# Feed-forward matmuls as two 64-row tiles of TensorE, two weight units at a time

## The chip, the core and the metric

The kernel runs on one core of a Trainium2 chip. The metric is the device time of one execution in microseconds (us). TensorE (PE) multiplies a stationary operand of up to 128 rows by 128 columns, loaded by an instruction of its own (LDWEIGHTS), with a moving operand of up to 512 columns; the result is added up in a bank of PSUM (2 KB per partition, here 512 float32). ScalarE (ACT) and VectorE (DVE) read the banks; GpSimd (POOL) works on SBUF only. SyncE (SP) issues the DMAs.

## The reference

Two layers, each: a SwiGLU feed-forward, a mixer of three attentions, a second SwiGLU feed-forward. There are 256 tokens of 1024 channels, and the inner width of the feed-forward is 2816.

```python
def swiglu(h, w1, w3, w2):
    return (jax.nn.silu(h @ w1) * (h @ w3)) @ w2
...
for l in range(DEPTH):
    x = x + 0.5 * swiglu(rms_norm(x, ffn1_norm[l]), ffn1_w1[l], ffn1_w3[l], ffn1_w2[l])
    ...                                   # mixer: projections, three branches, x = x + mixed @ w_out[l]
    x = x + 0.5 * swiglu(rms_norm(x, ffn2_norm[l]), ffn2_w1[l], ffn2_w3[l], ffn2_w2[l])
```

## The kernel before

**Weights.** All weights stream through one list of units of 1 MB (128 partitions x 2048 float32). A unit is loaded by SP into one of 3 `raw` buffers, and split into a high part `hl[:, 0]` (ACT, L138) and a low part `hl[:, 1]` (DVE, L144), in two halves, in one of 4 `hl` buffers. A product of float32 precision is then the sum of three matmuls: high by high, high by low, low by high. `unit()` takes the next unit of the list and makes sure that it and the first half of the next are split; `tick()` is called between pieces of matmul work and emits further splits (`fill`) and one step of each side task. Each engine runs its instructions in the order in which they were emitted.

**Feed-forward, first part (w1 and w3).** `fform(i)` does one unit: 128 columns of w1 and 128 of w3. The weights are stationary (128 rows of the contraction, 128 columns), the transposed activations `xT` move. For each of the two banks (b = 0 for w1, 1 for w3) and each of 8 blocks k of the contraction there are two matmuls: one of 512 columns (weights high, by the activations' high and low parts of all 256 tokens) and one of 256 columns (weights low, by the activations' high part). So a unit has 32 matmuls: 16 couples of 512 and 256 columns. `fdrain` then adds the two halves of each bank (ACT copy L478, DVE add L479), scales on POOL (L480), and in later ticks applies Silu (ACT L485), multiplies (DVE L487) and splits the result into high and low (ACT L489, DVE L491) as `uT`. In the very first feed-forward the units 0 and 1 are done elsewhere and `fform` runs from 2 to 21; in the other three, units 0 and 1 are done token by token (`tform`, then the transposes of `tr_task`), `fform` runs from 2 to 21 too, and after unit 2 `rs_bcast` transposes the norm's scale into a bank of tag `ta`.

**Feed-forward, second part (w2), and the mixer's output.** `wide_out` multiplies stationary activations (128 rows, 128 tokens) by moving weights (512 columns). For each unit u and each half t of the tokens, `wide_burst` does 12 matmuls of 512 columns into the two banks of t (h = 0, 1). The last two units are held back and done bank by bank, so that each bank finishes early. w2 has 11 units (9 in `wide_burst`, 2 held), the mixer's output 4 (2 and 2).

**PSUM.** Eight banks in two tags of four, given out in rotation: `acc` for the accumulators, `ta` for transposes and some others. `fform` takes two `acc` banks per unit, so that two units can be in flight.

Of the kernel before, what the change touches and what calls it, by code (L numbers as in the profile page):

```python
# [6 lines left out]
F32 = mybir.dt.float32  # L7
# [20 lines left out]
S2_BUFS = 31  # L28
FIRST_R = 2

# [15 lines left out]
def body(tc, T):  # L46
# [3 lines left out]
    with ctx:  # L50
# [21 lines left out]

# [1 line left out]
        units = []  # L74
# [95 lines left out]

# [1 line left out]
        tasks = []  # L172
# [28 lines left out]

# [1 line left out]
        x = cst.tile([128, 2, D], F32, name="x")  # L203
# [163 lines left out]
        def mm(out, lhsT, rhs, start, stop):  # L367
            PE.matmul(out=out, lhsT=lhsT, rhs=rhs, start=start, stop=stop, skip_group_check=True)  # L368

# [43 lines left out]
        def wide_out(first, lhs, nu, done):  # L413
            accs = {}
            hold = []
            for u in range(nu):
                hl = unit()
                if u >= nu - 2:
                    hold.append((u, hl))
                    continue  # L420
                for t in range(2):
                    if u == 0:
                        accs[t] = (acc_t(), acc_t())
                    wide_burst(accs[t], lhs, u, hl, t, u == 0, False)
                    tick()
            for t in range(2):
# [9 lines left out]

        def wide_burst(acc, lhs, u, hl, t, start, stop):
            for kk in range(2):
                s, e = start and kk == 0, stop and kk == 1
                for w in range(2):  # L440
                    for h in range(2):
                        mm(acc[h], lhs(0, u, kk, t), hl[:, w, kk * 1024 + h * 512:kk * 1024 + h * 512 + 512],
                           s and w == 0, False)
                for h in range(2):
                    mm(acc[h], lhs(1, u, kk, t), hl[:, 0, kk * 1024 + h * 512:kk * 1024 + h * 512 + 512], False, e)

# [1 line left out]
        def ffn(norms, after, prefetch, first=None, out=None):  # L448
# [44 lines left out]
            def fform(i):  # L493
                hl = unit()
                acc = [(at_t() if first is not None and i == 3 else acc_t()) for _ in range(2)]
                for b in range(2):
                    o = acc[b].rearrange("p (w t n) -> p w t n", w=2, t=2)
                    for k in range(8):
                        a = k * 256 + b * 128
                        both = xT[:, :, :, k, :].rearrange("p t w n -> p w t n")  # L500
                        mm(o, hl[:, 0, a:a + 128], both, k == 0, False)
                        mm(o[:, 0], hl[:, 1, a:a + 128], xT[:, :, 0, k, :], False, k == 7)
                    if b == 0:
                        tick()
                if i == (FIRST_R if first is not None else 2):
                    rs_bcast()
                    if first is not None:
                        for j in range(2):
                            drains[j] = run(fdrain(j, first[j][0][:, :256], first[j][1][:, :256]))
                        for j, a in held:  # L510
                            drains[j] = run(fdrain(j, a))
                if "x" in rs_b:
                    drains[i] = run(fdrain(i, acc))
                else:
                    held.append((i, acc))
                tick()

            us, drains, held = {}, {}, []
            if first is None:
                h2 = [unit(), unit()]  # L520
                for t in range(2):
                    finish(norms[t, 0])
                    finish(norms[t, 1])
                    for i in range(2):
                        us[i, t] = tform(i, h2[i], t)
                        tick(t == 0)
                utr = spawn(tr_task(us), 2)
            for i in range(2, NB):
                fform(i)
                if i == 4:  # L530
                    prefetch()
                    if first is not None:
                        load_consts()
                    if first is None:
                        finish(utr)

# [17 lines left out]

# [1 line left out]
        def mixer(l, norms, after, prefetch):  # L556
# [6 lines left out]

            # ---- evacuations of the projections
            sg, cn, rl, nqk, nav, gvt, ssr = {}, {}, {}, {}, {}, {}, {}
# [94 lines left out]

            # ---- shared by the two softmax attentions
            yT = {}
# [28 lines left out]

            # ---- neighbourhood attention
            naT = {}
# [89 lines left out]

            # ---- latent attention
            mq, mk, mv, mr = {}, {}, {}, {}
# [146 lines left out]

            # ---- gated linear attention
            gqk = {}
# [152 lines left out]

            # ---- projections, with the three mixers running beside them
            m_tk = dense8(512, ev_m, norms)
# [103 lines left out]

# [1 line left out]
        def spawner(ap, into, params_of=None):  # L1195
# [39 lines left out]
def _rel_index():  # L1235
    """Row offset, column offset and window test of (block, query, key) in the order of the bands."""
    j, q, p = np.arange(4)[:, None, None], np.arange(64)[:, None], np.arange(128)
# [102 lines left out]
```

## Time and profile before

| | us |
|---|---|
| median of 3 runs (1270.18 to 1270.63) | 1270.34 |
| span of the profiled execution, first to last instruction | 1267.6 |
| PE busy in it (share) | 1253.1 (99%) |
| PE weight loads busy | 1074.4 (85%) |
| DVE busy | 894.0 (71%) |
| ACT busy | 711.9 (56%) |
| POOL busy | 221.3 (17%) |

The profiled execution's own time is its span and what the runtime puts around it, which the profile does not show; the median of the runs is 2.7 us above the span. PE is busy almost throughout, but a matmul's record lasts longer than the step from it to the next one, since matmuls are pipelined: how fast PE goes is read from the starts of long groups of matmuls and their counts.

### The profile page before, as it was taken

How to read it: one execution, taken by the hardware profiler on the slowest of the kernel's cores; microseconds unless marked ns; L12 is line 12 of the kernel's file. 1: busy time of each engine (PE TensorE's matmuls, PEld its weight loads, DVE VectorE, ACT ScalarE, POOL GpSimd, SP SyncE). 2: the span in 40 equal slices, each digit the busy share in tenths (PEclk: the TensorE clock that was granted, in tenths of full speed). 3: DMA queues.
4: the chain of work that ended last, by engine and by line, in shares of the span. 5: the costliest groups of instructions: out<-in, count | busy, mean ns of one | idle time of the engine just before them, and what ended most of it. 6: DMA issues, size and time to landing. Idle time of an engine off the chain costs nothing.

```text
span 1267.6 us, 18330 instructions
## 1 busy us (share of the span) xinstructions
PE 1253.1 (99%) x7124; PEld 1074.4 (85%) x7124; DVE 894.0 (71%) x1382; ACT 711.9 (56%) x1315; POOL 221.3 (17%) x169
## 2 busy tenths in 40 slices
PE   8999999999999999999999999999999999999998
PEld 7888788889988898888898888888899788988887
DVE  5888736678766878886378886466886567788852
ACT  6555536667665366555365564356686644665541
POOL 0322101132011112220012220021322020122200
PEclk9999999999999999999999999999999999999999
DMA  7655644552543545556355556346526434555561
GB/s 301 222 180 187 241 158 158 203 194 87 196 166 133 200 166 185 185 196 232 133 186 203 195 195 235 113 173 225 167 90 207 163 134 170 196 199 182 186 230 34
DMA packets 37751, 228.34 MB, mean 180 GB/s; under 512 B 5712, under 2 KB 6864, under 8 KB 13088
## 3 DMA queue, kind: packets, MB, share of 16 engines
q1 hardware_dynamic: 37488, 227.09, 50.5%
q8 instruction: 56, 0.92, 0.3%
q14 instruction: 31, 0.25, 0.1%
q0 software_dynamic: 32, 0.07, 0.0%
q10 hardware_dynamic: 144, 0.00, 0.0%
HBM read 224.00 MB, written 1.05 MB: 178 GB/s over the span
## 4 chain that ended last, share of the span: by engine, by line
PE 88%; DVE 7%; ACT 4%; issue 1%; DMA 0%; DVEq 0%; ACTq 0%
PE acc L368 79%; DVE hl L144 6%; PE ta L368 6%; ACT hl L138 2%; ACT s L478 1%; PE ta L689 1%; PE ta L259 1%; DVE s L487 1%; PE ta L776 0%; DVE aT L1017 0%; PE ta L1172 0%; DMA gcol<-in_gcol 0%; PE ta L674 0%; ACT aT L1016 0%; PE ta L608 0%
## 5 line engine op out<-in xcount | busy, mean ns | idle before, releaser
L144 DVE TENSOR_TENSOR hl<-raw,hl 128x1024 fp32r<-128x1024 f32 (+2 forms) x422 | 568.0, 1385 | 101.7 <-ACT hl L138 91.4
L138 ACT ACTIVATE hl<-raw 128x1024 fp32r<-128x1024 f32 (+2 forms) x422 | 417.2, 1041 | 110.2 <-PE acc L368 93.5
L368 PE MATMUL acc<-xT,hl 128*128 128x512 f32 (+1 forms) x2768 | 475.6, 334 | 0.6 <-DVE s L479 0.6
L368 PEld LDWEIGHTS acc<-xT,hl 128*128 128x128 f32 x2768 | 417.8, 188 | 55.7 <-DVE s L479 0.9
L368 PE MATMUL acc<-hl,xT 128*128 128x512 f32 (+2 forms) x1728 | 369.0, 369 | 0.0
L368 PEld LDWEIGHTS acc<-hl,xT 128*128 128x128 f32 x1728 | 299.8, 188 | 45.7 <-issue 2.1
L368 PE MATMUL acc<-hl,s 128*128 128x512 f32 x1344 | 310.9, 391 | 1.5 <-DVE s L479 1.5
L368 PEld LDWEIGHTS acc<-hl,s 128*128 128x128 f32 x1344 | 250.8, 188 | 54.4 <-DVE s L479 1.9
L480 POOL TENSOR_TENSOR s<-s,rsb 128x512 f32<-128x512 f32 x80 | 111.8, 1397 | 355.7 <-DVE s L479 355.7
L489 ACT ACTIVATE s<-s 128x256 fp32r<-128x256 f32 x82 | 34.2, 418 | 172.4 <-DVE s L487 172.4
L479 DVE TENSOR_TENSOR s<-acc,s 128x256 f32<-128x256 f32 x158 | 59.6, 419 | 58.5 <-ACT s L478 58.5
L569 POOL TENSOR_TENSOR sm<-sm,mhalf 128x4 f32<-128x4 f32 (+2 forms) x24 | 36.7, 1531 | 202.7 <-DVE sm L573 196.0
L280 POOL TENSOR_TENSOR sm<-sm,mhalf 128x1 f32<-128x1 f32 x12 | 14.2, 1182 | 298.5 <-DVE sm L279 298.5
L478 ACT ACTIVATE s<-acc 128x256 f32<-128x256 f32 x158 | 50.6, 372 | 0.0
L242 ACT ACTIVATE s<-ta 128x512 fp32r<-128x512 f32 (+1 forms) x46 | 22.9, 531 | 39.9 <-PE ta L689 19.9
L243 DVE TENSOR_TENSOR s<-ta,s 128x512 fp32r<-128x512 f32 (+1 forms) x46 | 26.6, 604 | 24.4 <-ACT s L242 24.1
L368 PE MATMUL ta<-s,s 64*64 64x128 f32 (+3 forms) x720 | 41.0, 265 | 2.1 <-ACT s L1026 2.1
L368 PEld LDWEIGHTS ta<-s,s 64*64 64x64 f32 (+2 forms) x720 | 32.1, 144 | 12.4 <-issue 5.9
L262 ACT ACTIVATE xT<-ta,gain 128x128 fp32r<-128x128 f32 x80 | 22.8, 369 | 35.1 <-PE ta L259 35.1
L485 ACT ACTIVATE s<-s 128x256 f32<-128x256 f32 x82 | 34.2, 418 | 10.9 <-POOL s L480 0.2
L546 DVE SCALAR_TENSOR_TENSOR x<-acc,x 128x512 f32<-128x512 f32 (+1 forms) x20 | 11.3, 579 | 39.7 <-PE acc L368 39.7
L491 DVE TENSOR_TENSOR s<-s,s 128x256 fp32r<-128x256 f32 x82 | 34.0, 415 | 1.9 <-ACT s L489 1.9
(158 smaller groups left out, 652.4 us busy)
## 6 DMA issues: line engine op xcount, KB each, us to landing
raw<-in_l_f_w SPq DMA_DIRECT2D x130, 1024.0 KB, 4.8
raw<-in_l_in_g SPq DMA_DIRECT2D x16, 816.0 KB, 4.4
raw<-in_l_in_late SPq DMA_DIRECT2D x8, 1024.0 KB, 4.8
raw<-in_l_out SPq DMA_DIRECT2D x8, 1024.0 KB, 4.7
raw<-in_l_in_m SPq DMA_DIRECT2D x4, 1024.0 KB, 4.8
raw<-in_l_in_gr SPq DMA_DIRECT2D x4, 1024.0 KB, 4.8
raw<-in_l_in_r SPq DMA_DIRECT2D x4, 1024.0 KB, 4.8
raw<-in_l_in_nv SPq DMA_DIRECT2D x4, 1024.0 KB, 5.0
```

Of the source, the lines that this page charges most:

```text
L138: ACT.activation(out=hls[j][:, 0, sl], in_=raws[j][:, sl], func=AF.Copy)
L144: DVE.tensor_tensor(out=hl[:, 1, sl], in0=r[:, sl], in1=hl[:, 0, sl].bitcast(F32), op=ALU.subtract)
L242: ACT.activation(out=hi, in_=ps, func=AF.Copy)
L243: DVE.tensor_tensor(out=lo, in0=ps, in1=hi.bitcast(F32), op=ALU.subtract)
L368: PE.matmul(out=out, lhsT=lhsT, rhs=rhs, start=start, stop=stop, skip_group_check=True)
L478: ACT.activation(out=g[:, j, :], in_=a[j][:, 256:], func=AF.Copy)
L479: DVE.tensor_tensor(out=g[:, j, :], in0=a[j][:, :256], in1=g[:, j, :], op=ALU.add)
L480: POOL.tensor_tensor(out=g, in0=g, in1=rb[:, None, :].to_broadcast([128, 2, 256]), op=ALU.mult)
L485: ACT.activation(out=g[:, 0, :], in_=g[:, 0, :], func=AF.Silu)
L489: ACT.activation(out=o[:, 0, :], in_=g[:, 0, :], func=AF.Copy)
L491: DVE.tensor_tensor(out=o[:, 1, :], in0=g[:, 0, :], in1=o[:, 0, :].bitcast(F32), op=ALU.subtract)
L569: POOL.tensor_tensor(out=r[:, :n], in0=ss[:, :n], in1=mhalf[:, :n], op=ALU.pow)
```

## The change

`mm` now returns its instruction, and a new helper `duo(P, Q)` issues matmuls in halves: each matmul of 128 contraction rows becomes two of 64 rows, one on rows 0 to 63 and one on rows 64 to 127 of the array. P and Q are two lists of runs with banks of their own. In the first pass the lower row tile does P's runs and the upper one Q's, alternating instruction by instruction; in the second pass they change sides, so that every bank gets both halves of its contraction, and never from both tiles at once. Between the passes a POOL memset of one element (`dot`, L393) waits for the last matmuls of the first pass in a pair of banks, and the second pass there waits for the memset.

`fform_pair(i)` gives `duo` two units (i and i+1) with two banks each, four banks of one tag, `ta` and `acc` in turn. `wide_out` gives it the two token halves of one unit, for all units that are not held back, and swaps their order from unit to unit. In the first feed-forward units 2 and 3 stay with `fform`, and pairs run from 4; in the others from 2, and there `rs_bcast` and the transposes of `tr_task` now stand together behind the first pair. Ticks: four per pair (two per unit before), four per w2 unit (two before).

```diff
         def mm(out, lhsT, rhs, start, stop):
-            PE.matmul(out=out, lhsT=lhsT, rhs=rhs, start=start, stop=stop, skip_group_check=True)
+            return PE.matmul(out=out, lhsT=lhsT, rhs=rhs, start=start, stop=stop, skip_group_check=True).ins
+        HALF = (slice(0, 64), slice(64, 128))
+        dot = cst.tile([1, 4], F32, name="dot")
+        def duo(P, Q, between=None):
+            gate = {}
+            for second in (False, True):
+                for n, pair in enumerate(zip(*((Q, P) if second else (P, Q)))):
+                    last = [None, None]
+                    for i in range(len(pair[0][0])):
+                        for r in range(2):
+                            ops, start, stop = pair[r]
+                            out, lhsT, rhs = ops[i]
+                            last[r] = mm(out, lhsT[HALF[r]], rhs[HALF[r]], start and not second and i == 0,
+                                         stop and second and i == len(ops) - 1)
+                            if second and i == 0:
+                                tc.add_manual_dep(last[r], gate[n], SYNC, reason="the other row tile's run in this bank")
+                    if not second:
+                        g = POOL.memset(dot[:, n:n + 1], 0.0).ins
+                        for r in range(2):
+                            tc.add_manual_dep(g, last[r].name, SYNC, reason="both row tiles' runs")
+                        gate[n] = g.name
+                    if between is not None and not (second and n == len(P) - 1):
+                        between()
...
-                for t in range(2):
-                    if u == 0:
+                if u == 0:
+                    for t in range(2):
                         accs[t] = (acc_t(), acc_t())
-                    wide_burst(accs[t], lhs, u, hl, t, u == 0, False)
-                    tick()
+                P, Q = (wide_runs(accs[t], lhs, u, hl, t) for t in range(2))
+                duo(*((Q, P) if u % 2 else (P, Q)), between=tick)
+                tick()
...
+            def fform_pair(i):
+                runs, accs = [], []
+                for j in (i, i + 1):
+                    hl = unit()
+                    acc = [at_t() if i // 2 % 2 == 0 else acc_t() for _ in range(2)]
...
+                duo(*runs, between=tick)
+                if i == 2:
+                    rs_bcast()
+                    finish(utr)
+                for j in range(2):
+                    drains[i + j] = run(fdrain(i + j, accs[j]))
+                tick()
...
-            for i in range(2, NB):
-                fform(i)
+            if first is not None:
+                for i in (2, 3):
+                    fform(i)
+            for i in range(2 if first is None else 4, NB, 2):
+                fform_pair(i)
```

**Place 1, PE, second feed-forward of layer 0, behind the transposes of the norm's scale (`ta<-idt`).** Before, one bank of one unit after the other; a row is the line, the bank written, the two operands with their buffer numbers, and the output's size:

```order
L466 MATMUL ta_4399<-idt_73,s2_4350 128x128 [waits DVE_49]
L368 MATMUL acc_4416<-xT_74,hl_4251 128x512 [waits Activation_49]
L368 MATMUL acc_4416<-xT_74,hl_4251 128x256
L368 MATMUL acc_4416<-xT_74,hl_4251 128x512
L368 MATMUL acc_4416<-xT_74,hl_4251 128x256
```

Now, at the same place:

```order
L498 MATMUL ta_5387<-idt_73,s2_5231 128x128
L367 MATMUL ta_5410<-xT_74,hl_5236 128x512 [waits Activation_49]
L367 MATMUL ta_5415<-xT_74,hl_5275 128x512 [waits Activation_49]
L367 MATMUL ta_5410<-xT_74,hl_5236 128x256 [waits DVE_49]
L367 MATMUL ta_5415<-xT_74,hl_5275 128x256 [waits DVE_49]
L367 MATMUL ta_5410<-xT_74,hl_5236 128x512
L367 MATMUL ta_5415<-xT_74,hl_5275 128x512
```

Two units (`hl_5236`, `hl_5275`) and two banks alternate, each instruction with half the rows, and the second unit has to be split from the second instruction on.

**Place 2, PE, the first w2 unit of the same feed-forward.** Before, the two banks of one token half alternate:

```order
L368 MATMUL acc_5354<-xT_74,hl_5267 128x256
L368 MATMUL acc_5405<-hl_5319,s2_4404 128x512 [waits DVE_49]
L368 MATMUL acc_5406<-hl_5319,s2_4404 128x512 [waits DVE_49]
L368 MATMUL acc_5405<-hl_5319,s2_4404 128x512
L368 MATMUL acc_5406<-hl_5319,s2_4404 128x512
```

Now the passes; these are the end of the first pass and the start of the second:

```order
L367 MATMUL acc_6943<-hl_6774,s2_5395 128x512
L367 MATMUL acc_6945<-hl_6774,s2_5395 128x512
L367 MATMUL acc_6944<-hl_6774,s2_5392 128x512 [waits Pool_49]
L367 MATMUL acc_6942<-hl_6774,s2_5392 128x512
L367 MATMUL acc_6944<-hl_6774,s2_5392 128x512
```

The second pass of this unit begins with a wait for POOL, 24 instructions (two groups of six couples) behind the unit's start.

**Place 3, POOL, the end of w1/w3 and the start of w2 in the same feed-forward.** Before:

```order
L480 TENSOR_TENSOR s2_5295<-s2_5295,rsb_4393 128x512 [waits DVE_49,Pool_49]
L480 TENSOR_TENSOR s2_5347<-s2_5347,rsb_4393 128x512 [waits DVE_49,Pool_49]
L480 TENSOR_TENSOR s2_5399<-s2_5399,rsb_4393 128x512 [waits DVE_49,Pool_49]
L280 TENSOR_TENSOR sm_5808<-sm_5710,mhalf_81 128x1 [waits DVE_49]
```

Now:

```order
L393 MEMSET dot_84 1x1 [waits PE_49,Pool_49] x2
L512 TENSOR_TENSOR s2_6930<-s2_6930,rsb_5385 128x512 [waits DVE_49]
L512 TENSOR_TENSOR s2_6936<-s2_6936,rsb_5385 128x512 [waits DVE_49]
L393 MEMSET dot_84 1x1 [waits PE_49,Pool_49] x18
L279 TENSOR_TENSOR sm_7583<-sm_7485,mhalf_81 128x1 [waits DVE_49]
```

The memset that lets the first w2 unit's second pass start stands behind the scaling (L512, L480 before) of the last two w1/w3 units.

## Rows read from the trace of the kernel before

**Rows 1.** Page, part 1: engine, busy us, share of the span, instructions.
```profile
PE 1253.1 (99%) x7124; PEld 1074.4 (85%) x7124; DVE 894.0 (71%) x1382; ACT 711.9 (56%) x1315; POOL 221.3 (17%) x169
```

**Rows 2.** Waits of PE over the whole execution: us, times, longest.
```profile
PE ta L368 <- ACT hl L337: 6.0, 1, 6.0
PE ta L368 <- ACT s L1026: 2.1, 2, 1.1
PE acc L368 <- DVE s L479: 2.1, 2, 1.5
PE ta L1172 <- DVE s L1163: 0.4, 2, 0.2
```

**Rows 3.** Timeline of PE, 469 to 640 us: start, length, engine, group, count.
```profile
469.92 106.98 PE L368 MATMUL acc<-xT,hl 128*128 128x512 f32 x608
576.73 54.60 PE L368 MATMUL acc<-hl,s 128*128 128x512 f32 x240
631.17 0.60 PE L259 MATMUL ta<-idt,x 128*128 128x128 f32 x4
```

**Rows 4.** Timeline of PE, 426 to 457 us: the mixer's output.
```profile
430.96 14.20 PE L368 MATMUL acc<-hl,xT 128*128 128x512 f32 x60
445.00 0.60 PE L259 MATMUL ta<-idt,x 128*128 128x128 f32 x4
```

**Rows 5.** Windows, 470 to 576 us: busy (count) by engine, PEclk, DMA.
```profile
core 0: us, PE busy (x) PEld busy (x) DVE busy (x) ACT busy (x) POOL busy (x), PEclk, DMA share, GB/s
470.00:576.00 106.00, 106.00 (x606) 92.90 (x605) 88.49 (x114) 62.75 (x116) 26.39 (x19) 1.00 0.54 187
```

**Rows 6.** Timeline of PE, latent attention's scores; then two shorter stretches of it.
```profile
294.22 1.47 PE L368 MATMUL acc<-xT,hl 128*128 128x256 f32 x11
295.53 2.89 PE L368 MATMUL ta<-s,s 128*128 128x256 f32 x24
298.35 0.50 PE L368 MATMUL acc<-xT,hl 128*128 128x256 f32 x2
...
296.33 0.51 PE L368 MATMUL ta<-s,s 64*128 64x256 f32 x4
...
296.33 0.63 PE L368 MATMUL ta<-s,s 64*128 64x256 f32 x6
```

**Rows 7.** Timeline of PE, gated linear attention: a burst of 64 by 64 tiles.
```profile
1010.70 0.89 PE L368 MATMUL ta<-s,s 64*64 64x128 f32 x24
1011.52 3.05 PE L368 MATMUL acc<-hl,xT 128*128 128x512 f32 x12
```

**Rows 8.** Timeline of all engines, 576 to 582 us: the end of w1/w3.
```profile
576.77 0.64 ACT L478 ACTIVATE s<-acc 128x256 f32<-128x256 f32 x2
577.17 0.76 DVE L479 TENSOR_TENSOR s<-acc,s 128x256 f32<-128x256 f32 x2 [0.76 <-ACT s L478]
578.07 1.34 POOL L480 TENSOR_TENSOR s<-s,rsb 128x512 f32<-128x512 f32 x1 [4.21 <-DVE s L479]
```

**Rows 9.** Groups of POOL: busy us, mean ns of one.
```profile
L300 POOL MEMSET ones<- 128x1 f32 x1 | 0.1, 98 | 0.0
```

**Rows 10.** Timeline of PE, the first feed-forward's change from w1/w3 to w2.
```profile
44.15 90.14 PE L368 MATMUL acc<-xT,hl 128*128 128x512 f32 x512 [0.57 <-DVE s L479]
134.12 2.88 PE L368 MATMUL acc<-hl,s 128*128 128x512 f32 x12
138.49 52.07 PE L368 MATMUL acc<-hl,s 128*128 128x512 f32 x228 [1.49 <-DVE s L479]
```

**Rows 11.** Page, part 5: weight loads of two groups, mean ns in the middle.
```profile
L368 PEld LDWEIGHTS acc<-hl,s 128*128 128x128 f32 x1344 | 250.8, 188 | 54.4 <-DVE s L479 1.9
```

## What the change will do: the prediction

> **What bounds the kernel now.** The page first: PE is busy for 99% of the span, the next engine for 71% [rows 1]. The list of PE's waits confirms it: some 11 us in all, most of it once at the start [rows 2]. So the time is the number of matmuls times the step from one to the next, and the steps are what the change touches. They are read from starts in PE's timeline, not from busy time. In w1/w3 the 608 matmuls that start at 469.92 end where the next group starts, at 576.73 [rows 3]: 106.81 us for 304 couples of 512 and 256 columns, 0.3514 us a couple. In w2, 240 matmuls of 512 columns take 631.17 - 576.73 = 54.44 us, 0.2268 us each [rows 3]; in the mixer's output 60 take 14.04 us, 0.234 us each [rows 4]. The granted clock is 1.00 [rows 5], the 2.4 GHz level, at which 512 columns alone are 0.2133 us, a couple 0.3200. What is left above the columns is 13 to 21 ns per matmul, and no more than that can be gained in these stretches.
>
> How much of the kernel they are: pairs run 9 times in the first feed-forward and 10 times in each other one, 39 duos of 2 units of 16 couples, 1248 couples x 0.3514 = 438.5 us; w2 has 4 x 9 units of 24 matmuls, 864 x 0.2268 = 196.0 us; the mixers' outputs 96 x 0.234 = 22.5 us. Together 657 us.
>
> **The change, part by part.**
>
> *The step of a row-tiled matmul.* A matmul of 128 rows becomes two of 64 rows with the same columns. If the two run side by side, a slot (the two together) lasts as long as the one did, and nothing is gained in streaming. The trace has such matmuls already: in the latent attention's scores, 64 rows by 128 columns by 256 columns, in two row tiles and two banks. Four of them last 0.51 us from the first start to the last end, six last 0.63 [rows 6]: one more pair costs 0.12 us. Full-height matmuls of 256 columns right before take 295.53 - 294.22 = 1.31 us for 11, 0.119 us each [rows 6]. So two tiles do run side by side, and the step stays the same, gap included: 0.12 against 0.1067 for the columns alone. No row shows 512 columns in row tiles. I take the nearest row, the same matmul width of 128 columns at half the length, and so no change: 0 us. The bounds: the gap goes altogether (0.2133 and 0.3200, worth -52.9 us, worked out below), or all 512-column slots take the slowest step seen, 0.234 (w2: 864 x 0.0072 = +6.2 us; couples at 0.234 + 0.120: 1248 x 0.0026 = +3.2 us).
>
> *Twice the instructions.* There are 3456 more matmuls and as many loads. A slot now has four instructions in 0.176 us on average, 44 ns each. In the gated attention 24 matmuls with their loads start in 1011.52 - 1010.70 = 0.82 us, 17 ns each [rows 7], so issuing them is hidden behind streaming; 0 us. Loads do not bind either: the 256-column pair of tiles has two loads in its 0.12 us.
>
> *Going in and out of row tiling.* The same group of rows prices it. From 295.53 to 298.35, 2.82 us, PE does 12 full matmuls and 6 pairs in turns (6, 3, 6, 3): 18 slots of 0.12 are 2.16, the other 0.66 us are four changes of tiling, 0.165 us each [rows 6]. In the order the changed kernel has 11 row-tiled blocks: one in the first feed-forward, two in each other one (the pair of units 2 and 3, then transposes, then the rest through w2), two in each mixer's output, where transposes of the merge stand after the first quarter of unit 0. 22 changes x 0.165 = **+3.6 us**.
>
> *The gates.* In w1/w3 a pass is 2 x 16 slots, 16 couples or 5.62 us. The first gate's memset is queued on POOL behind the scaling of the two units of the pair before. At the end of w1/w3 (the group that starts at 576.73 [rows 3] is w2) the rows give: copies from 576.77, adds until 577.93, scaling from 578.07 for 1.34 us [rows 8], that is until 2.68 us behind the change. The second unit's copies and adds lie beside it and its scaling follows directly: until 4.02; a small memset is 0.1 us [rows 9]: 4.12 us. The second pass starts at 5.62 us, so in w1/w3 the gate is hidden with 1.5 us to spare. But behind the last pair comes w2, whose pass is only 12 slots x 0.2268 = 2.72 us, and the first unit's gate has the same two scalings ahead of it. PE waits 1.4 us, a little less where ACT is free earlier than in the rows: I take 1.3, four times: **+5.2 us**. All that is behind this matmul on PE waits with it; behind the memset on POOL stand only later memsets and the next norm's scale. From the second w2 unit on POOL has nothing else, the memset has the second bank's run of 6 slots, 1.36 us, for its 0.1 us: hidden. In the mixers' outputs POOL is free as well.
>
> *The wait at the end of the first feed-forward.* There the second token half of the first w2 unit waits 1.49 us for the add (L479) that empties its `acc` bank [rows 10]. With pairs the last units lie in `ta`, and `acc` was emptied a pair earlier: **-1.5 us**. The other wait, 0.57 us before unit 5, only changes its place: the first pair needs a `ta` bank of unit 3 at once.
>
> *Two units at once.* The second unit must be split one unit's time earlier, and the four `hl` buffers are freed in twos. DVE, the fuller of the two splitting engines, needs 88.49 us of 106 [rows 5], 9.4 of the 11.24 us of a pair; its first adds start with the pair and the last split is due at the next one's second quarter. The cover is nearly 2 us per pair, so 0 us; without it every microsecond late is 39 us in all. After the first pair of three feed-forwards the next one needs the bank of the scale's transposes, at most some 0.3 us each: inside the range.
>
> Sum: +3.6 + 5.2 - 1.5 = +7.3 us. The profiled span of 1267.6 us becomes 1274.9; the median of the runs is 2.7 us above the span, so the runs should show **1277.6 us**.
>
> **The rivals.**
>
> *The gap shrinks (faster).* If the 13 to 21 ns between matmuls are the weight switch, and one tile streams while the other switches, they may vanish: couples 1248 x (0.3514 - 0.3200) = 39.2, w2 864 x 0.0135 = 11.7, mixers 96 x 0.0207 = 2.0; 52.9 us less, 1224.7 us. For it speaks that each tile has its own load; against it the 0.12 us per pair of tiles, which still holds 13 ns above its columns. It decides from 2.8 ns per slot on: 3456 slots then give 9.8 us, which pays the 7.3 and 2.5 more. Chance 0.16. The Trainium skill ("TensorE: Matmul & The Clock Gate", section Part 3 on row and column tiling) says that a weight load overlaps running matmuls only when its row group differs; by it the tiles would hide loads that are bare today, and the time would fall as here or further. Today's trace disagrees: a load lasts 188 ns [rows 11] and the step of 512 columns is 0.2268 us, 13 ns over the columns, so loads of the same rows are hidden already, and this rule leaves only those 13 ns to gain.
>
> *The gap becomes even.* The couple's 0.3514 is 31 ns over its columns, two gaps of 13 ns would give 0.3467. The 256-column tiles show 13. If the 512-column ones do too: 1248 x 4.7 ns = 5.9 us and the mixers 0.7 us less, 1271.0 us, nothing to be measured. Chance 0.19.
>
> *The gates come late in every pair.* DVE's adds of a pair, if DVE runs behind, or the memsets' own waits could use up the 1.5 us. From there on each microsecond costs 39 us: 1317 us for one. Against it: POOL is busy 26.39 of 106 us [rows 5]. Chance 0.08.
>
> *No side by side at 512 columns.* Then 657 us are added, 1935 us. The pairs of 256 columns speak against it. Chance 0.03.
>
> **How the numbers follow.** The forecast has 0.54, with 1272.9 to 1288 for it alone (the bounds of the step; gates between nothing and 2 us). A measurement of this kernel tells 0.2%, 2.5 us, from no change. Faster is the first rival, 0.16; within 0.2% most of the second, 0.16; slower the forecast, the last two rivals and the rest of the second, 0.68. The range leaves out the last rival, most of the late gates and most of the first rival: it reaches down to a quarter of that one's gain, 1277.6 - 13 = 1264, and up past the slow steps (1287) with 5 us for gates: 1292.
>
> **What would show it.** PE's timeline of w1/w3 in row tiles: 0.351 us per couple slot means the step is right, 0.347 the even gap, towards 0.32 the first rival. A wait of PE for POOL's memset, four times and about 1.3 us, at the change from w1/w3 to w2, and none elsewhere; no wait for DVE's L511 there in the first feed-forward. Gaps of PE at the eleven blocks. Waits for POOL in each pair would be the third rival. The forecast is wrong if the step of 512 columns in row tiles moves by more than 3 ns either way.

## The result, and the profile after

The changed kernel takes 1290.53 us (median of 4 runs, 1288.04 to 1294.28) against 1270.26 us: ratio 1.0166 [1.0149, 1.0183]. The forecast was 1277.6 us, +7.3; measured is about +20. The sign was right, the size was not: 1290.53 lies just inside the range's upper end. The profiled execution took 1288.77 us, its span is 1287.0 us, 19.4 more than before's 1267.6, and its granted clock is 0.997 on average (1.000 before). The four runs spread by 6 us, and their granted clock with them, from 0.997 to 0.993.

The first part of the page and PE's waits in the changed kernel (us in all, times, longest); they answer to [rows 1, 2]:

```profile
PE 1263.2 (98%) x10580; PEld 1079.7 (84%) x10580; DVE 869.7 (68%) x1382; ACT 713.2 (55%) x1315; POOL 262.2 (20%) x327
```

```profile
PE acc L367 <- POOL dot L393: 7.2, 4, 1.8
...
PE ta L367 <- DVE hl L143: 2.4, 1, 2.4
...
PE ta L367 <- POOL dot L393: 0.9, 3, 0.3
PE ta L828 <- POOL s L822: 0.6, 1, 0.6
```

POOL's instructions nearly double (x169 to x327, the 158 memsets), PE's grow by 3456. The forecast waits for the memset are there, four times, but 1.8 us long instead of 1.3. A wait of 2.4 us for a low part of the weights (L143) was not forecast, and the three of 0.3 us behind the first pairs were called "inside the range". No wait is left for L511, the add that held up the first w2 before [rows 10].

PE's timeline of the changed kernel in the second feed-forward of layer 0 (start, length, group, count); it answers to [rows 3]:

```profile
469.71 11.48 PE L367 MATMUL acc<-xT,hl 64*128 64x512 f32 x128
...
481.92 5.87 PE L367 MATMUL ta<-xT,hl 64*128 64x512 f32 x64
488.10 5.87 PE L367 MATMUL ta<-xT,hl 64*128 64x512 f32 x64 [0.31 <-POOL dot L393]
493.81 11.36 PE L367 MATMUL acc<-xT,hl 64*128 64x512 f32 x128
505.01 11.36 PE L367 MATMUL ta<-xT,hl 64*128 64x512 f32 x128
...
583.41 2.92 PE L367 MATMUL acc<-hl,s 64*128 64x512 f32 x24
588.12 52.24 PE L367 MATMUL acc<-hl,s 64*128 64x512 f32 x432 [1.80 <-POOL dot L393]
640.20 0.60 PE L258 MATMUL ta<-idt,x 128*128 128x128 f32 x4
```

A pair of units takes 505.01 - 493.81 = 11.20 us for 32 couples: 0.3500 us a couple against 0.3514. From 588.12 to 640.20 w2 does 204 slots in row tiles and 24 full matmuls, 52.08 / 228 = 0.2284 us against 0.2268. So the tiles do run side by side, and streaming is what it was.

**Where the forecast gate went wrong** is in the timeline of all engines, same kernel, 583 to 588.2 us; it answers to [rows 8]:

```profile
583.41 2.92 PE L367 MATMUL acc<-hl,s 64*128 64x512 f32 x24
583.61 0.94 ACT L510 ACTIVATE s<-ta 128x256 f32<-128x256 f32 x3 [2.41 <-PE ta L367]
584.03 1.09 DVE L511 TENSOR_TENSOR s<-ta,s 128x256 f32<-128x256 f32 x3 [2.12 <-ACT s L510]
...
584.53 1.30 POOL L512 TENSOR_TENSOR s<-s,rsb 128x512 f32<-128x512 f32 x1 [6.35 <-DVE s L511]
585.52 1.39 DVE L143 TENSOR_TENSOR hl<-raw,hl 128x1024 fp32r<-128x1024 f32 x1 [0.41 <-ACT hl L137]
585.78 2.25 POOL L512 TENSOR_TENSOR s<-s,rsb 128x512 f32<-128x512 f32 x1
586.84 2.28 DVE L143 TENSOR_TENSOR hl<-raw,hl 128x1024 fp32r<-128x1024 f32 x1
...
587.98 0.12 POOL L393 MEMSET dot<- 1x1 f32 x2
```

The scalings start 1.1 us behind the change to w2, a little earlier than the 1.34 worked out. The first takes 1.30 us, as in [rows 8]; the second takes 2.25, and it is the same at all four changes to w2. What differs is which engine began first. The second scaling starts while DVE is at a low part of the weights (L143, from 585.52); the first starts before it. In [rows 8] a low part lies beside the scaling too, but it starts later, and there the low part is the longer one, 2.11 us instead of 1.21:

```profile
578.39 2.11 DVE L144 TENSOR_TENSOR hl<-raw,hl 128x1024 fp32r<-128x1024 f32 x1
```

All scalings bear this out. In the changed kernel the 40 that start while a low part runs take 2.18 to 2.30 us, the other 40 1.28 to 1.31; before, one of 80 starts so, at 31.26 us, and takes 2.21, the others 1.30 to 1.42. The Trainium skill ("SBUF — State Buffer", section "SBUF: two separate sides") says that GpSimd and a VectorE instruction with two inputs in SBUF, as the low part has, need the same pair of ports, and that the one that starts first holds it to its end while the other is blocked. The lengthened durations agree with that within 0.2 us. So the second pass starts 4.71 us behind the first one's start, whose 12 slots are 2.72: 1.99 us lost, four times 8.0.

**What no term held is the clock.** Windows of PE in the changed kernel around the 2.4 us wait (it ends at 35.34) and the last wait for the memset (it ends at 1223.75); PEclk is the granted clock:

```profile
core 0: us, PE busy (x), PEclk, DMA share, GB/s
34.00:36.70 2.70, 1.36 (x15) 1.00 0.84 349
36.70:40.15 3.45, 3.45 (x25) 0.51 0.77 264
40.15:46.00 5.85, 5.85 (x69) 1.00 0.43 139
1219.04:1224.57 5.53, 3.74 (x36) 1.00 0.29 123
1224.57:1227.99 3.42, 3.42 (x20) 0.50 0.66 180
1227.99:1240.00 12.01, 12.01 (x109) 1.00 0.71 250
```

Behind both, PE works for 3.4 us at half clock, the 1.2 GHz level. Behind the second, eight w2 slots start from 1224.55 to 1227.94 us, 0.423 us each instead of 0.227: 1.6 us lost; the first pair takes 12.7 us instead of 11.2, 1.5 lost. In this execution two of the five waits have such a drop. The spread of the runs fits two to five of them: 0.004 of the clock in 1290 us is 5 us, and the highest time is 6.2 above the lowest.

### The profile page after: what moved, and what is told of

Same layout as the page of the kernel before. It is cut to its first block, busy times and chain, and to the rows that moved or that the text cites. A ratio compares the mean times of both kernels' runs of the same rounds, so it can differ in the third digit from the quotient of the medians.

```text
span 1287.0 us, 25553 instructions
## 1 busy us (share of the span) xinstructions
PE 1263.2 (98%) x10580; PEld 1079.7 (84%) x10580; DVE 869.7 (68%) x1382; ACT 713.2 (55%) x1315; POOL 262.2 (20%) x327
## 4 chain that ended last, share of the span: by engine, by line
PE 91%; DVE 3%; ACT 2%; issue 1%; DMA 1%; POOL 1%; SPq 0%; DVEq 0%; ACTq 0%; POOLq 0%
PE acc L367 67%; PE ta L367 21%; DVE hl L143 2%; POOL s L512 1%; DMA raw<-in_l_f_w 1%; PE ta L741 1%; ACT hl L137 1%; PE ta L258 1%; DMA s<-in_l_bias 0%; PE ta L828 0%; DVE aT L1069 0%; DVE s L242 0%; DVE s L511 0%; PE ta L1224 0%; PE ta L726 0%
## 5 line engine op out<-in xcount | busy, mean ns | idle before, releaser
L143 DVE TENSOR_TENSOR hl<-raw,hl 128x1024 fp32r<-128x1024 f32 (+2 forms) x422 | 549.1, 1340 | 115.3 <-ACT hl L137 115.0
L367 PE MATMUL acc<-hl,xT 128*128 128x512 f32 (+3 forms) x1824 | 371.4, 371 | 0.0
L367 PEld LDWEIGHTS acc<-hl,xT 128*128 128x128 f32 (+1 forms) x1824 | 299.9, 188 | 48.7 <-issue 3.5
L367 PE MATMUL acc<-hl,s 64*128 64x512 f32 (+1 forms) x2208 | 314.3, 390 | 7.2 <-POOL dot L393 7.2
L367 PEld LDWEIGHTS acc<-hl,s 64*128 64x128 f32 (+1 forms) x2208 | 256.1, 186 | 58.3 <-POOL dot L393 8.9
L367 PE MATMUL ta<-xT,hl 64*128 64x256 f32 (+2 forms) x2640 | 244.9, 335 | 9.3 <-ACT hl L336 5.7
L367 PE MATMUL acc<-xT,hl 64*128 64x256 f32 (+2 forms) x2704 | 252.9, 329 | 0.4 <-DVE hl L143 0.4
L367 PEld LDWEIGHTS acc<-xT,hl 64*128 64x128 f32 (+1 forms) x2704 | 220.6, 184 | 28.4 <-DVE hl L143 0.6
L367 PEld LDWEIGHTS ta<-xT,hl 64*128 64x128 f32 (+1 forms) x2640 | 210.5, 186 | 40.1 <-ACT hl L336 6.0
L512 POOL TENSOR_TENSOR s<-s,rsb 128x512 f32<-128x512 f32 x80 | 141.3, 1789 | 270.7 <-DVE s L511 270.7
L393 POOL MEMSET dot<- 1x1 f32 x158 | 13.5, 88 | 270.1 <-PE acc L367 248.7
L511 DVE TENSOR_TENSOR s<-ta,s 128x256 f32<-128x256 f32 x82 | 30.7, 417 | 41.3 <-ACT s L510 41.3
L511 DVE TENSOR_TENSOR s<-acc,s 128x256 f32<-128x256 f32 x78 | 29.0, 417 | 36.0 <-ACT s L510 36.0
```

The source lines that it names most:

```text
L143: DVE.tensor_tensor(out=hl[:, 1, sl], in0=r[:, sl], in1=hl[:, 0, sl].bitcast(F32), op=ALU.subtract)
L367: return PE.matmul(out=out, lhsT=lhsT, rhs=rhs, start=start, stop=stop, skip_group_check=True).ins
L511: DVE.tensor_tensor(out=g[:, j, :], in0=a[j][:, :256], in1=g[:, j, :], op=ALU.add)
L512: POOL.tensor_tensor(out=g, in0=g, in1=rb[:, None, :].to_broadcast([128, 2, 256]), op=ALU.mult)
```

## The experiments

The theory after the result: the slowdown is mostly waits of PE (the first pair's, the four gates) and the clock behind them (**waits theory**). Rival A: row tiles cost it themselves. Rival B: two units at once, whatever the rows.

### Full rows in the changed order

`duo` with one pass over all 128 rows:

```diff
-                for n, pair in enumerate(zip(*((Q, P) if second else (P, Q)))):
+            for n, pair in enumerate(zip(P, Q)):
...
+                        mm(out, lhsT, rhs, start and i == 0, stop and i == m - 1)
```

> The changed kernel's order, pairs and ticks, but each matmul with all 128 rows again, so no row tiles, no second pass and no memsets. Waits theory (the slowdown is PE's waits, 2.4 us before the first pair and four of 1.8 us for the memsets, plus 3.4 us at half clock behind two of them): the first pair's wait stays with its clock drop, the rest goes; before + 2.4 + 1.7 - 0.6 - 1.5 (the removed wait) - 1.7 (shorter couples, if it is the order that shortens them), 1269 to 1273 us. Rival A (row tiles themselves cost it, by slots, changes of tiling and their power): 1268 to 1273 as well. Rival B (two units at once, or the new order of ticks and banks, costs it in w1/w3, w2 and the mixers alike): 1280 us or more.

Measured: 1275.59 us, ratio 1.0044 [1.0029, 1.0059]. 15 of the 20 us go with the row tiles and their gates. The time lies between the sums, 3 us above the waits theory's and 4 below rival B's. The profile has the first pair's wait (2.34 us) with a drop behind it, a new wait of 1.8 us in the second mixer, and mixers that are 1 us longer. PE's timeline of this kernel, and its two longest waits behind the start:

```profile
490.55 11.47 PE L367 MATMUL acc<-xT,hl 128*128 128x512 f32 x64
501.86 11.47 PE L367 MATMUL ta<-xT,hl 128*128 128x512 f32 x64
```

```profile
PE ta L367 <- DVE hl L143: 2.3, 1, 2.3
...
PE ta L816 <- POOL s L810: 1.8, 1, 1.8
```

A pair takes 11.31 us, 0.3534 us a couple: with full rows the changed order (two units in turn, over four banks) is slower than before, and row tiles only give that back.

### Row tiles in w1/w3 alone, and in w2 and the mixers' outputs alone

First `wide_burst` of before in `wide_out`:

```diff
-                P, Q = (wide_runs(accs[t], lhs, u, hl, t) for t in range(2))
-                duo(*((Q, P) if u % 2 else (P, Q)), between=tick)
-                tick()
+                    wide_burst(accs[t], lhs, u, hl, t, u == 0, False)
+                    tick()
```

> Row tiles in w1/w3 alone; w2 and the mixers' outputs as before. Waits theory: the four waits for the memset at the start of w2 go, the first pair's wait with its half clock stays: before + 4.1 - 0.6 - 1.5 - 1.7 + 14 changes of tiling at 0.165 = 2.3, about 1273 us, one clock drop. Rival A (row tiles cost by their share of the matmuls, 2496 of 3456 slots): 14 of the 20 us, about 1284 us.

Measured: 1276.81 us, 1.0055 [1.0038, 1.0071]. The four waits for the memset are gone and the first pair's is there, as the theory has it; 3.8 us are missing from its sum, of which the mixers, here with code as before, are 2. Rival A's 1284 is out.

The other half, before's `fform` with `duo` in `wide_out`:

```diff
-                    wide_burst(accs[t], lhs, u, hl, t, u == 0, False)
-                    tick()
+                P, Q = (wide_runs(accs[t], lhs, u, hl, t) for t in range(2))
+                duo(*((Q, P) if u % 2 else (P, Q)), between=tick)
```

> Row tiles in w2 and the mixers' outputs alone; w1/w3 unit by unit as before. Waits theory: no first pair; the gate of the first w2 unit stands behind one scaling, not two (2.8 us against the pass of 2.7), so at most 0.3 us each, but both token halves need their banks at the start, two of them still being emptied, about 1.2 us each in four places (more in the first feed-forward, 4 us): before + 1.4 (slots) + 2.6 (16 changes of tiling) + 1.8 (mixers' outputs) + 5 to 8 = 1281 to 1284 us. Rival A (row tiles by share, 960 of 3456 slots): 1276 us.

Measured: 1277.72 us, 1.0063 [1.0048, 1.0078]: too low for the theory's sum. Rival A's 1276 lies at the lower edge of the interval; it is the run before that speaks against it. In the first feed-forward PE waits 2.9 us for a bank at the first w2, with a clock drop behind it; in the other three there is no such wait, which is where 4 us were expected in vain. The halves give +7.0 and +7.9 of the 20: the long gates need both, pairs (two scalings) ahead of a w2 in row tiles.

### The waits taken away

In `fdrain` the last pair's scaling waits three ticks, and pairs of the first feed-forward run from 6 (the single unit 5 lies in `ta`, like unit 3):

```diff
+                    if i >= NB - 2:
+                        yield 3
                     POOL.tensor_tensor(out=g, in0=g, in1=rb[:, None, :].to_broadcast([128, 2, 256]), op=ALU.mult)
...
-                for i in (2, 3):
+                for i in (2, 3, 4, 5):
                     fform(i)
-            for i in range(2 if first is None else 4, NB, 2):
+            for i in range(2 if first is None else 6, NB, 2):
```

> All row tiles kept; the scaling of the last pair is issued three ticks later, behind the first w2 unit's two memsets, and in the first feed-forward units 4 and 5 go one by one and pairs run from 6. Waits theory: the four waits of 1.8 us, the first pair's 2.4 us and the two clock drops (1.7 us each) go: 1288.8 - 7.2 - 2.4 - 3.4 = 1275.8 us, granted clock 1.000, and a smaller spread of the runs. Rival A (row tiles themselves): 1283 to 1288 us.

Measured: 1278.58 us, 1.0067 [1.0052, 1.0082]; 12 us of the 20 are gone with all row tiles kept but those of one pair. The four gates don't wait any more. The first pair still does, in two pieces of 1.0 and 1.6 us, and has its clock drop, which more than covers the 2.8 us by which the sum missed. PE's waits in this kernel:

```profile
PE acc L367 <- DVE hl L143: 2.0, 2, 1.6
...
PE acc L367 <- ACT hl L137: 1.0, 1, 1.0
PE ta L367 <- POOL dot L393: 0.9, 3, 0.3
```

### A second profile of before

> The kernel before once more, for a second profile. In the changed kernel and in all of the four experiments the two mixers take about 1 us each longer from residual to residual than the profiled execution of before (254.59 and 254.65 us), also where their code is that of before. If that is how executions differ: span near 1269.5 us and mixers of about 255.6 us. If the change does it: 254.6 us again.

Measured: 1270.53 us, span 1268.8. The transposes that open and close the first mixer stand at 191.05 and 445.89, so it takes 254.84 us, 0.25 more than in the first profile. The mixers' extra 1 us is the change's.

### Longer waits

In `fdrain`, ahead of the scaling:

```diff
+                    if i == NB - 1:
+                        POOL.tensor_tensor(out=s2((128, 2, 256)), in0=g, in1=rb[:, None, :].to_broadcast([128, 2, 256]), op=ALU.mult)
```

> The changed kernel with one more scaling on POOL ahead of the first w2 unit's memset (its result is not used). Clock theory (a wait of PE of some 2 us is followed now and then, a longer one always, by 3.4 us at half clock, 1.7 us lost each): the four waits grow from 1.8 to about 3.5 us, +6.8 us, and each has its clock drop, five with the first pair's instead of two, +5.1 us: about 1300.7 us, granted clock 0.993. Rival (the two drops of the changed kernel have nothing to do with the waits): 1295.6 us, clock 0.997.

Measured: 1304.05 us, 1.0269 [1.0255, 1.0283], granted clock 0.989. PE's wait in this kernel and windows around two of the four:

```profile
PE acc L367 <- POOL dot L393: 16.0, 4, 4.0
```

```profile
145.40:148.80 3.40, 3.40 (x20) 0.51 0.65 270
...
590.36:594.36 4.00, 0.00 (x2) 0.78 0.12 14
594.36:599.40 5.04, 5.04 (x24) 0.50 0.51 197
599.40:605.00 5.60, 5.60 (x52) 1.00 0.71 214
```

All four waits, now 4.0 us, have a drop, and three of them a longer one that starts within the wait. Behind the waits PE works 3.4, 5.0, 5.8 and 5.5 us at half clock, 3.4 more behind the first pair: 23.1 against 6.8 us in the changed kernel. At 1.6 us per 3.4, those 16.3 us more cost 7.7; with 16.0 - 7.2 = 8.8 us of longer waits that is 16.5, measured 16.2 in the span. The rival is out.

### Pairs later in the first feed-forward, and row tiles in one block

The single units' odd ones lie in `ta` here and in the next run.

```diff
-                for i in (2, 3, 4, 5):
+                for i in range(2, 10):
                     fform(i)
-            for i in range(2 if first is None else 6, NB, 2):
+            for i in range(2 if first is None else 10, NB, 2):
```

> As the run with the late scaling, but in the first feed-forward units 2 to 9 go one by one and pairs run from 10, so that the splitting has more time to get a unit ahead. Waits theory: the two waits left at the first pair (1.0 and 1.6 us) and the clock drop behind them go: 1278.6 - 2.6 - 1.7 = 1274.3 us, clock 1.000. Rival (the splitting doesn't gain on PE in that stretch, and the first pair waits wherever it stands): 1278 us.

Measured: 1278.01 us, 1.0060 [1.0046, 1.0074]. The rival holds: the first pair waits 0.8 and 1.6 us at 66 us instead of at 44, with its drop. By unit 10 the splitting has not got ahead of PE. One of the four runs has a granted clock of 1.000 and takes 1276.33 us, 1.7 less than the others: that fits an execution without the drop, of which no trace is kept.

The same with one block of row tiles in each feed-forward, and `wide_burst` for the mixers' outputs (`nu == 4`):

```diff
+                if nu == 4:
+                    for t in range(2):
+                        wide_burst(accs[t], lhs, u, hl, t, u == 0, False)
...
+            for i in range(2, 4 if first is None else 10):
+                fform(i)
...
+            for i in range(4 if first is None else 10, NB, 2):
```

> As the run with pairs from 10, but in each feed-forward the row tiles are one block: units 2 and 3 of the other three go one by one with the transposes between them, pairs run from 4, and the mixers' outputs have full rows. 8 changes of tiling instead of 22, no gate of 0.31 us behind a first pair. Theory (a change of tiling costs 0.165 us): 1274.3 - 2.3 - 0.9 - 0.8 (what is left of the mixers' outputs) = 1270.3 us, as before. If the row tiles themselves were a gain, 1268 us or less; if each still costs, 1273 us or more.

Measured: 1276.65 us, 1.0053 [1.0039, 1.0066], 1.4 us below the run before, not the expected 4: at the new first pairs PE waits 0.5 us for a low part, three times. What a change of tiling costs is shown better by PE's timeline of the changed kernel in the mixer's output, where transposes with full rows stand between:

```profile
432.48 0.60 PE L1224 MATMUL ta<-idt,s 128*128 128x128 f32 x4
433.01 1.67 PE L367 MATMUL acc<-hl,xT 64*128 64x512 f32 x12
434.61 0.66 PE L1224 MATMUL ta<-idt,s 128*128 128x128 f32 x4
435.20 15.94 PE L367 MATMUL acc<-hl,xT 64*128 64x512 f32 x108
450.97 0.60 PE L258 MATMUL ta<-idt,x 128*128 128x128 f32 x4
```

From 432.48 to 450.97 are 18.49 us; the same stretch with full rows, from the next run (same places of the buffers), is 449.04 - 431.33 = 17.71. Four changes for 0.78 us, 0.19 each.

### The place of the buffers

First before with the little tile, then the changed kernel with the tile in a pool `dp` of its own, the last one in SBUF:

```diff
+        dot = cst.tile([1, 4], F32, name="dot")
+        POOL.memset(dot, 0.0)
```

> The kernel before with the changed kernel's little tile dot (16 bytes a partition) in its place, written once by one memset and otherwise not used. It moves every raw, hl and s2 buffer by 32 bytes, from multiples of 64 bytes to 32 above one. The mixers take 254.8 us in both profiles of before and 255.6 to 257.6 in all kernels with dot, also where their code is that of before. If it is the 32 bytes: mixers of 255.6 us here too, about 1272 us in all. If it is something else in the changed program (banks, ticks, its length): 254.8 us and 1270.3 us.

Measured: 1271.03 us, 1.0011 [1.0003, 1.0020], 1.3 us above before, where about 2 were expected. The profiled execution, 1273.21 us, is the slowest of its eleven and has a wait of 1.74 us with a clock drop at the first w2. PE's timeline of this kernel:

```profile
193.29 0.60 PE L259 MATMUL ta<-idt,x 128*128 128x128 f32 x4
...
431.33 0.60 PE L1175 MATMUL ta<-idt,s 128*128 128x128 f32 x4
...
449.04 0.60 PE L259 MATMUL ta<-idt,x 128*128 128x128 f32 x4
...
473.89 106.65 PE L368 MATMUL acc<-xT,hl 128*128 128x512 f32 x608
580.39 1.78 PE L368 MATMUL acc<-hl,s 128*128 128x512 f32 x7
```

The first mixer takes 449.04 - 193.29 = 255.75 us, 0.9 more than in the second profile of before: the little tile alone, with one memset, does it. But w1/w3 gains by it: 106.50 us for 304 couples, 0.3503 instead of 0.3514.

```diff
-        dot = cst.tile([1, 4], F32, name="dot")
+        dot = dp.tile([1, 4], F32, name="dot")
```

> The changed kernel with dot in a pool of its own behind the others, so that raw, hl and s2 lie where they lay before. If the 32 bytes cost time: mixers about 1 us faster each, 1288.5 us (a few us more or less as more or fewer of the five waits have a clock drop behind them). If not: 1290.5 us.

Measured: 1290.80 us, 1.0169 [1.0155, 1.0183], no better than the changed kernel. The mixers are 0.8 us faster each, w1/w3 and the rest of the feed-forwards lose nearly as much again (0.35 us each), and this profile has four clock drops where the other has two. PE's windows behind the second gate of this kernel, which had no drop in the changed kernel, and its timeline at the start of the third pair and at the start of w2:

```profile
585.38:587.18 1.80, 0.00 (x0) 1.00 0.00 0
588.70:592.10 3.40, 3.40 (x20) 0.50 0.88 289
592.10:600.00 7.90, 7.90 (x72) 1.00 0.74 274
```

```profile
492.58 11.40 PE L368 MATMUL acc<-xT,hl 64*128 64x512 f32 x128
...
582.46 2.92 PE L368 MATMUL acc<-hl,s 64*128 64x512 f32 x24
```

With the buffers where they were, eight pairs in row tiles take 582.46 - 492.58 = 89.88 us, 0.3511 a couple: 0.3 ns under before.

### All of it, and the one part that pays

First the run with one block per feed-forward again, late scaling and all, but with no pairs in the first one, and with `dot` in the pool `dp`:

```diff
-            for i in range(2, 4 if first is None else 10):
+            for i in range(2, 4 if first is None else NB):
                 fform(i)
-            for i in range(4 if first is None else 10, NB, 2):
+            for i in range(4 if first is None else NB, NB, 2):
```

> As the run with one block of row tiles per feed-forward, with dot in a pool of its own, and with the first feed-forward's w1/w3 unit by unit (odd units in ta, even ones in acc), its w2 in row tiles. Theory (the first pair's two waits and its clock drop, and the 32 bytes): no wait of PE over 1.1 us and no clock drop; 1276.7 - 2.4 - 1.7 - 1.5 = 1271 us; the old wait for the add at the first w2 goes too, so 1270 us can be. If the 32 bytes cost nothing: 1272.5 us. If row tiles have a cost of their own left: 1273 us or more.

Measured: 1271.30 us, 1.0014 [1.0005, 1.0023], granted clock 1.000 and no wait of PE over 1.1 us behind the start. With the waits out of the way the kernel is only 1.6 us above before. But this is not the row tiles' own cost, since the odd units in `ta` gain something by themselves; the next run has them without row tiles.

Then before with one line of `fform` changed, so that odd units of the first feed-forward lie in `ta`:

```diff
-                acc = [(at_t() if first is not None and i == 3 else acc_t()) for _ in range(2)]
+                acc = [(at_t() if first is not None and i % 2 else acc_t()) for _ in range(2)]
```

> The kernel before, with the odd units of the first feed-forward's w1/w3 in ta banks, the even ones in acc, and nothing else changed: no row tiles, no pairs. It takes over the one part of the change that should pay. Theory: the waits of 0.6 us before unit 5 and of 1.5 us at the first w2 unit, both for a bank being emptied, go and nothing comes in their place: 1269.7 - 2.1 = 1267.6 us, faster than both kernels. Rival: the splitting, which is hardly faster than PE there, is late next, and PE waits for it instead: 1269.7 us.

Measured: 1266.62 us, 0.9975 [0.9966, 0.9985], 3.4 us below before and faster than the changed kernel. Neither of the two waits for a bank is left in its list of waits; a wait of 0.5 us for a low part is there, as one of 0.4 is in the second profile of before. Of the 3.4 us, 2.1 were expected from these waits; where the other 1.3 lie stays open.

Against this run, the run above shows what row tiles, with their pairs and the late scaling, still cost. The transposes that end the first mixer and the second feed-forward of layer 0, first there, then here:

```profile
442.13 0.60 PE L259 MATMUL ta<-idt,x 128*128 128x128 f32 x4
...
629.66 0.60 PE L259 MATMUL ta<-idt,x 128*128 128x128 f32 x4
```

```profile
442.22 0.60 PE L259 MATMUL ta<-idt,x 128*128 128x128 f32 x4
...
628.40 0.60 PE L259 MATMUL ta<-idt,x 128*128 128x128 f32 x4
```

With row tiles this feed-forward takes 187.53 us, without them 186.18. The same 1.4 us appear in each of the three feed-forwards with pairs, and nothing in the first; the spans differ by 4.0 us.

## Why the prediction was right in its sign and wrong in its size

| term of the sum | forecast | measured | from |
|---|---|---|---|
| step in row tiles | 0 | -1.7 | couples 0.3500; of this -1.4 is the place of the buffers |
| 22 changes of tiling | +3.6 | +4.2 | 0.19 each in the mixer's output |
| gates at w2's start | +5.2 | +8.0 | 4 x 1.99 |
| wait for the add removed | -1.5 | -1.5 | not in the list |
| two units at once | 0 | +1.8 | 2.39 us, less the 0.57 of before |
| gates behind `rs_bcast` | 0 (in the range) | +0.9 | 3 x 0.31 |
| granted clock | none | +3.1 | 1.5 and 1.6 behind 2 waits; more in slower runs |
| place of the buffers, mixers | none | +1.8 | 2 x 0.9 |
| second mixer's wait for L822 | none | +0.6 | list of waits |

The measured terms add up to 17.2 of the 19.4 us. w2's 228 slots, 0.2284 for 0.2268, hold another 1.5 in four places, of which the change of tiling at their end is 0.7 and counted above. Some 1.4 us are not assigned.

**The steps that failed.** The 12 us that the sum missed do not come from one step. The first is that a wait was priced at its own length: no term held the clock, +3.1 us here and more in the slower runs. In the profiles of this study all ten waits of PE of 2.3 us or more behind the start have half clock in or behind them, and five of the ten between 1.74 and 1.82 us; the shorter ones that stand alone have none (1.49 us in [rows 10], 1.55 in the second profile of before), but the first pair's two pieces of 0.8 to 1.0 and 1.6 us do, three times of three. The Trainium skill ("TensorE: Matmul & The Clock Gate", section Part 1) says that this clock follows how busy the engine has been, and these counts agree. Gates of 1.3 us, as forecast, would by these counts have had no drop: the clock came with waits that were longer than forecast.

**The second** is the gate, 8.0 us for 5.2: the mechanism, the place and the count were right, but "its scaling follows directly" gave the second unit's scaling the 1.34 us of the first. It starts while a low part of the weights is running, and takes 2.25. The trace of before has one scaling of that kind, 2.21 us at 31.26. Taking the gates' waits away in the run with the late scaling shortened these feed-forwards by 2.1 us each.

**The third** is "the cover is nearly 2 us per pair, so 0 us" for two units at once: the first pair waits 2.39 us for a low part, and a drop follows. The cover was worked out from busy time in the second feed-forward, where the splitting is ahead (and there it holds: no wait from 493.81 to 583.41). In the first feed-forward it is not ahead, and the runs with pairs from 6 and from 10 show that it had not become so by then.

That +7.3 had the right sign is not luck: the changes of tiling and the gates are there. That 1290.53 us still lies in the range is: the range's upper end was made of slow steps, and the steps were not slow.

**The rivals.** *The gap shrinks* and *the gap becomes even* are out: at equal places of the buffers the couple is 0.3503 with full rows unit by unit and 0.3500 in row tiles. *Gates late in every pair*: only behind the first pairs, 0.3 us. *No side by side*: out. The test that the forecast set itself, 3 ns either way in the 512-column step, came out at 1.6. What it said of the later w2 units and of the mixers' outputs, no wait for the memset, holds too.

## What to carry to other kernels

Splitting full-height matmuls into row tiles wins nothing where loads are hidden already; what it brings is waits and changes of tiling, and in this kernel a wait of TensorE of 1.8 to 2.4 us cost up to nearly its own length again in clock. A cover read off in one stage holds for that stage: look at each stage, here the first feed-forward. Price an instruction by a row with the same neighbours on the other engines, and look at which of the two started first. A new small tile can move the large ones, and change steps that have nothing to do with it.

## What the runs showed of the hardware that was not expected

- A tile of 16 bytes a partition ahead of all `raw`, `hl` and `s2` buffers changes the step of full-rate matmuls: each mixer +0.9 us in 255, couples of w1/w3 -1.1 ns. That it is the shift of 32 bytes fits the run with the tile in its own pool, but no profile shows addresses, and which buffer does it was not tried.
- A scaling on GpSimd that starts while DVE is at a low part of the weights takes 2.2 to 2.3 us, one that starts before it 1.3 to 1.4. In the kernel before, the low part that starts during a scaling takes 2.1 us instead of 1.2.
- With the same full-height matmuls, alternating two units over four banks takes 0.3534 us a couple, bank by bank 0.3503, at equal places of the buffers.
- Drops of the clock are not the same from run to run: behind the same four waits of 1.8 us there is one in one profile, three in another.
